# A streaming-encoder block on one core: one more of eight weight pieces per FFN group by seven products, and some down weights' low parts made by accumulating transfers

## The chip, the core and the metric

The kernel runs on one core of a Trainium2 chip. The metric is device time in microseconds, the median of several executions. One further execution is recorded by the hardware profiler; it gives the trace from which all rows here are copied. Engines: PE is TensorE (matrix products; PEld its weight loads), DVE is VectorE, ACT is ScalarE, POOL is GpSimd, SP is SyncE, which here issues the loads. An engine's name with a q is its queue of DMA issues.

## The reference

One layer over 256 tokens with 2048 features, all in float32:

```python
for l in range(DEPTH):
    x = x + 0.5 * swiglu(rms_norm(x, ffn1_norm[l]), ffn1_w_up[l], ffn1_w_down[l])
    h = rms_norm(x, mix_norm[l])
    proj = h @ w_in[l]
    ...
    x = x + merged @ w_out[l]
    x = x + cross_attention(rms_norm(x, xattn_norm[l]), rms_norm(mem, mem_norm[l]),
                            xattn_wq[l], xattn_wkv[l], xattn_wo[l])
    x = x + 0.5 * swiglu(rms_norm(x, ffn2_norm[l]), ffn2_w_up[l], ffn2_w_down[l])
return rms_norm(x, final_norm)

def swiglu(h, w_up, w_down):
    gate, up = jnp.split(h @ w_up, 2, axis=-1)
    return (jax.nn.silu(gate) * up) @ w_down
```

The change concerns the two FFNs (`swiglu`): 2048 features to 2 x 5632 columns, and 5632 back to 2048.

## The kernel before

**Split operands.** A float32 matrix operand is used as two float32r parts: the high part is a rounded copy (`split`, line 120, on ScalarE) and the low part the difference from the original (line 121, on VectorE). A product of two such operands is made of three TensorE products, high by high, low by high and high by low (`three`, lines 449, 450 and 452).

**Groups and pieces.** The 5632 hidden columns are 11 groups of 512. The up weights of a group come in eight pieces of 1 MB (128 x 2048), one for each pair of feature tiles; a piece holds four blocks of 512 columns: two feature tiles, each with its up and its gate columns. A piece is used in one of these ways (`PRODUCTS`):
- plain (group 0): eight block products by three, 24 TensorE products;
- mixed: also eight block products, added into the same sums as the fast pieces;
- fast: seven block products (21 TensorE products) in the manner of Winograd's form of Strassen's scheme. VectorE first makes differences of the blocks into a tile `td` (lines 213 to 215), ScalarE copies three blocks of the piece and four of `td` to float32r, and VectorE makes the low parts (`l`, and `tl` in two halves).

The activations have matching sums and differences (`operand_pairs` and `sums`): "less" for a mixed pair, "sums" for a fast one, and both for the pairs in `BOTH`.

The down weights of a group are four pieces of 24 products. After each group's up pieces stand down pieces of earlier groups: two after groups 1 and 2, four after groups 3 to 10 (two blocks of two output columns: c0 b0, c0 b1, c1 b0, c1 b1, and likewise c2, c3 after the next group), and eight at the end (`ffn_order`). Groups 3 to 10 have the same pattern of 12 pieces and are called steady groups here.

**How a piece gets ready** (`weights`, `begin_added`, `prepare`). The list `plan` holds every piece in order of use. Each call of `weights` prepares the piece after the one that TensorE is about to use. `prepare` loads the piece into `raw` and splits it. A mixed piece with the kind "added" takes another way: its load is issued one piece earlier, ScalarE writes the negated rounded copy into `l` (line 191), and GpSimd issues a transfer that adds `raw` to `l` (line 192). So VectorE has nothing to do for it, ScalarE two passes, and the raw buffer stays taken until that transfer has landed. Before the change the kind "added" goes to the mixed pieces from group 3's second on, 15 in each FFN.

**Buffers.** `raw`, `h` and `l` are rings of three buffers; a fast piece takes two of `h` (the copies of the piece and of `td`). `td`, `tl` and the group's sums `ev` share a ring of three ("wide"). A buffer is written again when all uses of its last content are done. TensorE's sums are in eight banks.

**End of a group** (in `ffn`). Seven sums are put together from the banks: a copy on ScalarE (line 533), then seven additions on VectorE (lines 534 to 545), two SiLUs on ScalarE (line 481) and two products with the up part on VectorE (line 482). Four pieces later the result is transposed on TensorE (`turn`, line 489), copied and split. A pair of down pieces ends with two residual sums (line 561).

**Order.** Every engine has one instruction stream, in which a scheduler puts the instructions when the kernel is built; within an engine that order is fixed, and each instruction waits for its operands and buffers. In the first eight pieces the order is that of the code (`manual_schedule`); there `head` and `rest` hang other work behind certain pieces: loading x, the sums of squares for the first normalisation (`head_residual`, `sq1`, line 352), its square root (`head_rstd`), and the sums for the activations.

Of the kernel before, what the change touches and what calls it, by code (L numbers as in the profile page):

```python
# [13 lines left out]
P = 128  # L14
# [5 lines left out]
NG = DFF // 512  # L20
# [21 lines left out]
def ffn_order():  # L42

    out, down = [("plain", 0, p) for p in range(8)], [("down", 0, 1, c, 0) for c in range(4)]
    for g in range(1, NG):
        if g < 3:  # L50
            out += [(("mixed", "fast")[p % 2], g, p) for p in (0, 1, 2, 3, 5, 4, 7, 6)]
        else:
            out += [("mixed" if p in (0, 6) else "fast", g, p) for p in (1, 3, 0, 4, 2, 6, 5, 7)]
        if g > 2 and g % 2:
            down = [("down", g - 2, 2, c, b) for c in range(4) for b in (g - 2, g - 1)]
        n = 2 if g < 3 else 4
        out, down = out + down[:n], down[n:]
    return out + [("down", NG - 2, 2, c, b) for c in range(4) for b in (NG - 2, NG - 1)]
# [3 lines left out]
def block_kernel(ctx: ExitStack, tc: tile.TileContext, xT, xin, memT, vec, gfin, bgate, lruw, wu1, wd1, win, wv,  # L62
                 wg, wab, wout, wq, wk, wvm, wo, wu2, wd2, out_):
    nc = tc.nc
    pe, dve, act, sp = nc.tensor, nc.vector, nc.scalar, nc.sync
# [21 lines left out]
    def slot(dt=F32, name="slot"):  # L87
        return slots.tile([P, 1024], dt, name=name, tag="slot")
# [12 lines left out]
    def col(name, i=0, n=1):  # L101
        a = VEC[name][0] + i
        return vt[:, a:a + n]
# [8 lines left out]
    xt = [const.tile([P, 4 * T], F32, name=f"x{q}") for q in range(4)]  # L112
# [6 lines left out]
    def split(h, l, raw):  # L119
        done["high"] = act.activation(h, raw, ACT.Copy).ins  # L120
        dve.tensor_tensor(out=l, in0=raw, in1=h.bitcast(F32), op=ALU.subtract)  # L121
# [4 lines left out]

    plan, ahead = [], []
    orders = dict.fromkeys(("ffn1", "ffn2"), ffn_order())

    def plan_ffn(name, wu, wd):  # L130
        for e in orders[name]:
            src = wd[e[4], e[3]] if e[0] == "down" else wu[e[1], e[2]]
            kind = "fast" if e[0] == "fast" else "added" if e[0] == "mixed" and e[1:] > (3, 0) else "plain"
            plan.append(((name,) + e, src, kind))

    def plan_columns(name, w, which):
# [2 lines left out]
    def plan_rows(name, w, g):  # L139
        plan.extend(((name, g, kq), w[g, kq], "plain") for kq in range(w.shape[1]))  # L140

    plan_ffn("ffn1", wu1, wd1)
    for hf in range(2):
        for base in (8, 0):
# [11 lines left out]
    for name, w in (("mv", wvm), ("o", wo)):  # L156
        for g in range(4):
            plan_rows(name, w, g)
    plan_ffn("ffn2", wu2, wd2)

    head, rest = [], {}
# [238 lines left out]

    BOTH = [2, 4]
    xd = []

    def operand_pairs(src, gain, q, xg, out):

        for a in src:
            i = len(out)
            g = xg[:, i * 512:(i + 1) * 512]  # L410
            for z in range(2):
                act.activation(g[:, z * T:][:, :T], a[:, z * T:(z + 1) * T], ACT.Copy,
                               scale=col(gain, 4 * q + 2 * i + z))
            h, l = slot(F32R, "xh"), slot(F32R, "xl")
            split(h[:, :512], l[:, :512], g)
            less = None if i else (h[:, 512:768], l[:, 512:768])
            if 2 * q + i in BOTH:
                if 2 * q + i == BOTH[0]:
                    xd.append(slot(F32R, "xd"))
                n = 512 * BOTH.index(2 * q + i)  # L420
                less = [xd[-1][:, a:a + 256] for a in (n, n + 256)]
            out.append(((h, l), less))

        def sums(which=((0, "less"), (0, "sums"), (1, "less"), (1, "sums"))):
            s = slot(name="xs")
            for i, ((h, l), less) in enumerate(out):
                a = [xg[:, i * 512 + j * P:][:, :P] for j in range(4)]

                def made(h, l, n, at, terms):
                    o = [s[:, at + j * P:][:, :P] for j in range(n)]  # L430
                    for j, (x, y, op) in enumerate(terms(o)):
                        dve.tensor_tensor(out=o[j], in0=x, in1=y, op=op)
                    split(h, l, s[:, at:at + n * P])

                if less and (i, "less") in which:
                    made(*less, 2, 0, lambda o: ((a[0], a[1], ALU.subtract), (a[2], a[3], ALU.subtract)))
                if (i or 2 * q in BOTH) and (i, "sums") in which:
                    if not i and len(which) > 1:
                        s = slot(name="xs")
                    made(h[:, 512:], l[:, 512:], 4, 512 * i,  # L440
                         lambda o: ((a[1], a[3], ALU.add), (o[0], a[0], ALU.subtract),
                                    (a[1], a[0], ALU.subtract), (a[2], o[1], ALU.subtract)))

        return sums
# [126 lines left out]
    pairs1, sq1 = [], TokenSquares()  # L571

    xq, sums1 = {}, []

    def head_x(p):

        q = p // 2
        if p % 2 == 0:
            xq[q] = slot(name="xf"), slot(name="xg"), []
        src, xg, out = xq[q]  # L580
        a = p % 2 * 512
        sp.dma_start(src[:, a:a + 512], xT[:, p * 512:(p + 1) * 512])
        sums = operand_pairs([src[:, a:a + 512]], "ffn1_norm", q, xg, out)
        if p % 2:
            sums1.append(sums)
        pairs1.append(out[-1])

    def head_residual(i):
        for c in (2 * i, 2 * i + 1):
            for t in range(2):  # L590
                sp.dma_start(xt[c][:, t * 512:(t + 1) * 512], xin[t * P:(t + 1) * P, c * 512:(c + 1) * 512])
            sq1.add(c)
        if i:
            sp.dma_start(vt[:, small_n:NVEC], vec[:, small_n:])

    head += [lambda p=p: head_x(p) for p in range(8)]
    for i in range(2):
        rest[4 + i] = lambda i=i: head_residual(i)
    rstd1 = []

    def head_rstd():
        rstd1.append(sq1.rstd_tokens())
        act.activation(rstd1[0][:, 2:], rstd1[0][:, :1], ACT.Silu)

    for q, i in enumerate((3, 6, 7, 9)):
        rest[i] = lambda q=q: sums1[q](((0, "less"), (1, "sums")))
    rest[8] = head_rstd
    for q, i in ((1, 17), (2, 18)):
        rest[i] = lambda q=q: sums1[q](((0, "sums"),))


# [415 lines left out]
    for g in range(4):  # L1027
# [4 lines left out]
        for t in range(2):  # L1032
            s = slot(F32R, "vs")
            f = scoped["tmp2"].tile([P, 512], F32, name="vf", tag="part")
# [18 lines left out]
    def to_ffn(c):  # L1053
        out = []
        sums2.append(operand_pairs(turned(xt[c]), "ffn2_norm", c, slot(name="xg"), out))
        pairs2.extend(out)
        if c < 2:
            sums2.pop(0)()
# [130 lines left out]
```

## Time and profile before

| | |
|---|---|
| median of 3 runs | 2455.01 us (2454.0 to 2455.87) |
| profiled execution | 2456.57 us, its span in the trace 2454.8 us |
| TensorE, VectorE, ScalarE busy | 99%, 77%, 57% of the span |
| granted TensorE clock, mean | 0.997 |
| HBM read | 472.07 MB |
| adding transfers (line 192) | 30, median 7.3 us from issue to landing |

In a row of the timeline the columns are start, duration, engine, line, operation, output and inputs, and in brackets the engine's idle time before it with what ended it. A group's row gives busy time, the mean of one in ns, and the idle time in front. x with a number counts instructions. Records of products overlap: the spacing of their starts tells their cost. Windows give busy time of each engine in a stretch.

### The profile page before, as it was taken

The numbers are of one execution on the slowest core, as the hardware profiler recorded it, in microseconds if no ns is written. First come the engines' busy times: TensorE is split into PE (matmuls) and PEld (weight loads), VectorE is DVE, ScalarE is ACT, GpSimd is POOL, SyncE is SP. The second block draws the span as 40 slices with busy tenths as digits, with TensorE's granted clock in tenths as the row PEclk, the third lists the DMA queues.
The fourth block names the chain that finished last, engine by engine and source line by source line (L and its number), as shares of the span: only waits on it lengthen the run. The fifth ranks groups of instructions, "written<-read, shape, count | busy, mean of one in ns | idle before, by whom it ended". The sixth has DMA issues, their size and how long they took to land.

```text
span 2454.8 us, 30191 instructions
## 1 busy us (share of the span) xinstructions
PE 2434.6 (99%) x12250; PEld 2036.9 (83%) x12250; DVE 1894.1 (77%) x2016; ACT 1391.2 (57%) x1398; POOL 28.3 (1%) x36
## 2 busy tenths in 40 slices
PE   9999999999999999999999999999999999999998
PEld 7887888888888888888888888888888788888887
DVE  6998999999865757567665676556689999999995
ACT  7555666666564454477434554555555566666664
POOL 0000000000000000000000000000000000000000
PEclk9999999999999999999999999999999999999999
DMA  7557777777655445546555555444555677777774
GB/s 278 190 203 234 248 235 235 234 239 239 223 183 194 173 172 180 174 166 228 194 188 177 210 198 189 172 172 155 189 189 189 209 238 239 240 240 235 235 235 152
DMA packets 75020, 507.59 MB, mean 207 GB/s; under 512 B 8320, under 2 KB 8576, under 8 KB 15232
## 3 DMA queue, kind: packets, MB, share of 16 engines
q1 hardware_dynamic: 69840, 473.06, 53.4%
q0 software_dynamic: 4320, 31.46, 6.4%
q8 instruction: 96, 1.57, 0.2%
q10 hardware_dynamic: 720, 1.13, 0.1%
q14 instruction: 44, 0.36, 0.0%
HBM read 472.07 MB, written 2.10 MB: 193 GB/s over the span
## 4 chain that ended last, share of the span: by engine, by line
PE 95%; DVE 2%; ACT 1%; DMA 1%; issue 0%; SPq 0%; ACTq 0%; DVEq 0%
PE acc L449 17%; PE acc L450 17%; PE acc L452 17%; PE acc L231 11%; PE acc L252 8%; PE acc L253 8%; PE acc L255 8%; PE acc L235 5%; DMA raw<-wu 1%; PE acc L489 1%; ACT h L120 1%; DVE l L121 1%; PE acc L389 1%; PE acc L765 0%; PE acc L1048 0%; PE acc L1003 0%
## 5 line engine op out<-in xcount | busy, mean ns | idle before, releaser
L121 DVE TENSOR_TENSOR l<-raw,h 128x2048 fp32r<-128x2048 f32 (+2 forms) x422 | 878.0, 2087 | 364.5 <-ACT h L120 353.0
L120 ACT ACTIVATE h<-raw 128x2048 fp32r<-128x2048 f32 (+2 forms) x422 | 736.7, 1753 | 637.5 <-PE acc L253 204.8
L449 PE MATMUL acc<-h,xh 128*128 128x512 f32 x1280 | 501.2, 392 | 7.1 <-ACT h L120 7.0
L450 PE MATMUL acc<-h,xl 128*128 128x512 f32 x1280 | 499.7, 391 | 0.0
L120 ACT ACTIVATE h<-td 128x1024 fp32r<-128x1024 f32 x224 | 229.6, 1055 | 178.4 <-PE acc L450 131.0
L252 PE MATMUL acc<-h,ops 128*128 128x512 f32 x832 | 326.9, 393 | 0.0
L253 PE MATMUL acc<-h,ops 128*128 128x512 f32 x832 | 324.3, 390 | 0.0
L121 DVE TENSOR_TENSOR tl<-td,h 128x1024 fp32r<-128x1024 f32 x224 | 267.4, 1221 | 33.6 <-ACT h L120 31.0
L449 PEld LDWEIGHTS acc<-h,xh 128*128 128x128 f32 x1280 | 241.7, 189 | 60.0 <-ACT h L120 9.7
L450 PEld LDWEIGHTS acc<-h,xl 128*128 128x128 f32 x1280 | 241.9, 189 | 50.1
L231 PE MATMUL acc<-ops,h 128*128 128x512 f32 x1152 | 278.0, 393 | 0.3
L449 PE MATMUL acc<-h,hidop 128*128 128x512 f32 x704 | 275.7, 392 | 0.0
L450 PE MATMUL acc<-h,hidop 128*128 128x512 f32 x704 | 274.3, 390 | 0.0
L231 PEld LDWEIGHTS acc<-ops,h 128*128 128x128 f32 x1152 | 211.9, 188 | 42.9 <-DVE ops L292 0.9
L452 PE MATMUL acc<-l,xh 128*128 128x512 f32 x832 | 218.9, 390 | 0.0
L255 PE MATMUL acc<-l,ops 128*128 128x512 f32 x832 | 206.1, 390 | 0.0
L452 PE MATMUL acc<-l,hidop 128*128 128x512 f32 x704 | 188.3, 389 | 0.0
L452 PEld LDWEIGHTS acc<-l,xh 128*128 128x128 f32 x832 | 156.5, 188 | 32.6
L255 PEld LDWEIGHTS acc<-l,ops 128*128 128x128 f32 x832 | 156.2, 188 | 32.4
L252 PEld LDWEIGHTS acc<-h,ops 128*128 128x128 f32 x832 | 156.2, 188 | 32.3
L253 PEld LDWEIGHTS acc<-h,ops 128*128 128x128 f32 x832 | 156.3, 188 | 31.6
L452 PEld LDWEIGHTS acc<-l,hidop 128*128 128x128 f32 x704 | 132.2, 188 | 27.5
(220 smaller groups left out, 2347.6 us busy)
## 6 DMA issues: line engine op xcount, KB each, us to landing
raw<-wu SPq DMA_DIRECT2D x172, 1024.0 KB, 4.8
raw<-wd SPq DMA_DIRECT2D x88, 1024.0 KB, 4.8
raw<-win SPq DMA_DIRECT2D x40, 1024.0 KB, 4.8
raw<-wg SPq DMA_DIRECT2D x32, 1024.0 KB, 4.8
l<-raw POOLq DMA_DIRECT2D x30, 1024.0 KB, 7.3
raw<-wab SPq DMA_DIRECT2D x16, 1024.0 KB, 4.8
raw<-wout SPq DMA_DIRECT2D x16, 1024.0 KB, 4.8
raw<-wq SPq DMA_DIRECT2D x16, 1024.0 KB, 4.8
```

Source lines behind the costliest of these rows:

```text
L120: done["high"] = act.activation(h, raw, ACT.Copy).ins
L121: dve.tensor_tensor(out=l, in0=raw, in1=h.bitcast(F32), op=ALU.subtract)
L231: pe.matmul(acc, h[:, k * P:(k + 1) * P], xs[k], start=k == 0, stop=False)
L235: done["product"] = pe.matmul(acc[:, :T], l[:, k * P:(k + 1) * P], xs[k][:, :T], start=False, stop=k == KT - 1).ins
L252: pe.matmul(accs[t], x[:, t * P:][:, :P], h[j], start=first and j == 0, stop=False)
L253: pe.matmul(accs[t], x[:, T + t * P:][:, :P], h[j], start=False, stop=False)
L255: done["product"] = pe.matmul(accs[t], x[:, t * P:][:, :P], l[j], start=False, stop=last and j == 3).ins
L389: pe.transpose(accs[m // 2][:, m % 2 * T + t * P:][:, :P], tile[:, t * 512 + m * P:][:, :P], ident)
L449: pe.matmul(acc, ah, bh, start=start, stop=False)
L450: pe.matmul(acc, al, bh, start=False, stop=False)
L452: pe.matmul(acc, ah, bl, start=False, stop=stop)
L489: pe.transpose(acc[:, z * T + t * P:][:, :P], hid[t][:, (2 * y + z) * P:][:, :P], ident)
```

## The change

In groups 1 and 2 of each FFN pair 4 turns from mixed to fast (mixed are then 0, 2 and 6), in groups 3 to 10 pair 0 (mixed is then only 6, and it stands fourth). The kind "added" goes to every mixed piece but pair 0 and to two down pieces in each four behind groups 3 to 10: the first and the last of the four. `BOTH` names pairs 0 and 2, and pair 4, now only fast, has its sums where its "less" was. The order of loads into the ring of three follows `begin_added` as before. In the first pieces the residual's four chunks are loaded and squared one behind each of pieces 4 to 7 instead of two behind each of pieces 4 and 5, and the sums for the activations move.

```diff
-            out += [(("mixed", "fast")[p % 2], g, p) for p in (0, 1, 2, 3, 5, 4, 7, 6)]
+            out += [("mixed" if p in (0, 2, 6) else "fast", g, p) for p in (0, 1, 2, 3, 5, 4, 7, 6)]
         else:
-            out += [("mixed" if p in (0, 6) else "fast", g, p) for p in (1, 3, 0, 4, 2, 6, 5, 7)]
+            out += [("mixed" if p == 6 else "fast", g, p) for p in (1, 3, 0, 6, 4, 2, 5, 7)]
...
-            kind = "fast" if e[0] == "fast" else "added" if e[0] == "mixed" and e[1:] > (3, 0) else "plain"
+            kind = "fast" if e[0] == "fast" else "plain"
+            if e[0] == "mixed" and e[2]:
+                kind = "added"
+            if e[0] == "down" and 0 < e[1] < NG - 2 and (e[3] + e[4] - e[1]) % 2 == 0:
+                kind = "added"
...
-    BOTH = [2, 4]
+    BOTH = [0, 2]
+    FAST = [4]
...
-            less = None if i else (h[:, 512:768], l[:, 512:768])
+            less = None if i or 2 * q in FAST else (h[:, 512:768], l[:, 512:768])
...
-                if (i or 2 * q in BOTH) and (i, "sums") in which:
-                    if not i and len(which) > 1:
+                if (i or 2 * q in BOTH + FAST) and (i, "sums") in which:
+                    if not i and less and len(which) > 1:
...
-    def head_residual(i):
-        for c in (2 * i, 2 * i + 1):
-            for t in range(2):
-                sp.dma_start(xt[c][:, t * 512:(t + 1) * 512], xin[t * P:(t + 1) * P, c * 512:(c + 1) * 512])
-            sq1.add(c)
-        if i:
+    def head_residual(c):
+        for t in range(2):
+            sp.dma_start(xt[c][:, t * 512:(t + 1) * 512], xin[t * P:(t + 1) * P, c * 512:(c + 1) * 512])
+        sq1.add(c)
+        if c == 3:
...
-    for i in range(2):
-        rest[4 + i] = lambda i=i: head_residual(i)
...
-    for q, i in enumerate((3, 6, 7, 9)):
-        rest[i] = lambda q=q: sums1[q](((0, "less"), (1, "sums")))
-    rest[8] = head_rstd
-    for q, i in ((1, 17), (2, 18)):
+    for i in range(3):
+        rest[4 + i] = lambda i=i: head_residual(i)
+    for q, i in enumerate((3, 7, 8, 9)):
+        rest[i] = lambda q=q: sums1[q](((0, "sums" if 2 * q in FAST else "less"), (1, "sums")))
+    made = rest[7], rest[8]
+    rest[7] = lambda: [f() for f in (lambda: head_residual(3), made[0])]
+    rest[8] = lambda: [f() for f in (head_rstd, made[1])]
+    for q, i in ((0, 22), (1, 24)):
         rest[i] = lambda q=q: sums1[q](((0, "sums"),))
```

## The prediction

> **What bounds the kernel now.** I read the page first (busy times, then the chain of work that ended last), then the waits of TensorE, then stretches of one group of the FFN.
>
> ```profile
> span 2454.8 us, 30191 instructions
> PE 2434.6 (99%) x12250; PEld 2036.9 (83%) x12250; DVE 1894.1 (77%) x2016; ACT 1391.2 (57%) x1398; POOL 28.3 (1%) x36
> ...
> PE 95%; DVE 2%; ACT 1%; DMA 1%; issue 0%; SPq 0%; ACTq 0%; DVEq 0%
> ...
> PE acc L449 <- ACT h L120: 7.0, 4, 3.0
> PE acc L452 <- DVE tl L121: 3.0, 1, 3.0
> ```
>
> TensorE is busy 2434.6 of 2454.8 us and waits only 10 us for anybody: products set the end, so taking products away pays unless another engine takes over. VectorE's 77% hides two kinds of stage. The stretches below (columns: time, PE, weight loads, VectorE, ScalarE, GpSimd, then granted clock, DMA share, GB/s) show FFN groups 1, 2 and a steady group, each cut at its transposes:
>
> ```profile
> 61.62:114.45 52.83, 52.83 (x237) 43.54 (x236) 52.43 (x64) 29.93 (x28) 0.00 (x0) 1.00 0.56 199
> 114.45:166.35 51.90, 51.90 (x235) 43.06 (x233) 50.71 (x50) 27.64 (x24) 0.00 (x0) 1.00 0.55 203
> ...
> 286.57:348.67 62.10, 62.10 (x280) 51.50 (x278) 57.35 (x56) 38.38 (x32) 1.76 (x2) 1.00 0.73 237
> ...
> 286.57 1.03 PE L489 MATMUL acc<-vt,ev 128*128 128x128 f32 x8
> ...
> 348.67 1.03 PE L489 MATMUL acc<-vt,ev 128*128 128x128 f32 x8
> ```
>
> In the FFN VectorE works 92 to 99% of the time, so it is a near second bound there. The added FFN work lands on it; that decides this case.
>
> **The change part by part.** *Products.* Each group from 1 to 10 of both FFNs has one mixed piece (24 products) fewer and one fast piece (21) more. A steady group is 6x21 + 2x24 + 4x24 = 270 products and eight transposes. Taking about 0.8 us for the transposes (1.03 less the overlap of the last with what follows), (62.10 - 0.8)/270 = 0.227 us a product (the 0.39 us of one record is latency; they overlap). Three fewer are 0.68 us a group: a floor of 61.42 us, and 20 x 0.68 = 13.6 us in all if nothing else happens.
>
> *VectorE in a steady group (3 to 10).* The groups of its instructions in one period (393.19 to 455.28, columns busy, mean ns, idle before):
>
> ```profile
> L121 DVE TENSOR_TENSOR tl<-td,h 128x1024 fp32r<-128x1024 f32 x12 | 14.2, 1221 | 2.2 <-ACT h L120 2.0
> L121 DVE TENSOR_TENSOR l<-raw,h 128x1536 fp32r<-128x1536 f32 x6 | 10.5, 1756 | 1.3 <-PE acc L452 0.7 <-ACT h L120 0.6
> L121 DVE TENSOR_TENSOR l<-raw,h 128x2048 fp32r<-128x2048 f32 x4 | 9.1, 2288 | 0.9 <-ACT h L120 0.9
> L213 DVE TENSOR_TENSOR td<-raw 128x1024 f32<-128x1024 f32 x6 | 7.3, 1218 | 0.0
> L215 DVE TENSOR_TENSOR td<-raw,td 128x512 f32<-128x512 f32 x6 | 4.1, 691 | 0.2
> L214 DVE TENSOR_TENSOR td<-raw,td 128x512 f32<-128x512 f32 x6 | 4.1, 690 | 0.1
> ...
> ACT h L120 <- PE acc L450: 19.8, 12, 3.9
> ```
>
> A fast piece costs 1.22 + 0.69 + 0.69 + 1.76 + 2x1.22 = 6.8 us; the mixed piece it replaces was an adding transfer and cost VectorE nothing. Two of four down pieces become adding transfers: minus 2 x 2.29 = 4.6. So 57.4 + 6.8 - 4.6 = 59.6 us busy against a floor of 61.42: 1.8 us is left, where the group before had 2.2 + 1.3 + 0.9 + 0.3 = 4.7 us of idle.
>
> *A new wait at the group's end.* The weights' copies come from rings of three buffers. With the added down pieces the order is down A, P, P, A. The negated copy of the second A reuses the low buffer of the first A, so it waits until TensorE has ended the first A. In the changed kernel's instruction order on ScalarE this copy stands behind the group's first eviction and ahead of the high copy for the second P and of both SiLUs, and on VectorE the two gate products that need the SiLUs stand ahead of the second P's low part. The durations from the group's end before:
>
> ```profile
> 397.16 0.39 PE L449 MATMUL acc<-h,hidop 128*128 128x512 f32 x1
> ...
> 399.88 0.39 PE L449 MATMUL acc<-h,hidop 128*128 128x512 f32 x1
> ...
> 397.60 0.68 DVE L534 TENSOR_TENSOR ev<-acc,ev 128x512 f32<-128x512 f32 x1
> ...
> 401.92 1.41 DVE L482 SCALAR_TENSOR_TENSOR ev<-ev,rtok 128x512 f32<-128x512 f32 x2
> ...
> 399.17 1.92 ACT L120 ACTIVATE h<-raw 128x2048 fp32r<-128x2048 f32 x1 [3.72 <-PE acc L450]
> ...
> 400.99 1.32 ACT L481 ACTIVATE ev<-ev,rtok 128x512 f32<-128x512 f32 x2
> ...
> 411.06 1.90 ACT L191 ACTIVATE l<-raw 128x2048 fp32r<-128x2048 f32 x1
> ```
>
> Half a down piece is 2.72 us (397.16 to 399.88). Let E be the end of the group's last up product; TensorE's order puts the first half of the first A ahead of it, so that piece ends at E+2.7. Allowing 0.2 us for a wait to pass on: negated copy to E+4.8, high copy to E+6.7, first SiLU to E+7.4. VectorE starts its seven eviction sums at E+0.2, needs 4.3 us (397.60 to 401.92) and is done at E+4.5: it stands still for 2.9 us. Gates to E+8.8, low part of the second P (2.2) to E+11.0. TensorE needs it after the first P and eight products: E + 2.7 + 5.45 + 1.8 = E+9.95. It stalls 1.1 us. Behind the waiting copy on ScalarE also queue the high copies of the next group, behind the gates on VectorE its residual sums and differences.
>
> Two ways of counting meet: TensorE 61.42 + 1.1 = 62.5, VectorE 59.6 + 2.9 = 62.5. That is the lower end. The upper end keeps all 4.7 us of the old idle as well: 67.2. I take 0.9 of the 4.7: 3.5 was ended by ScalarE's copies, and ScalarE itself had waited 19.8 us for TensorE to release buffers; when VectorE is the late one these releases come early, and only the passing to and fro stays. So 63.4 us a group, 1.3 over before, in 16 groups: +20.8 us (ends: +0.4 and +5.1 a group).
>
> *Groups 1 and 2.* Of four mixed pieces three leave VectorE (two by adding transfers, one as fast): +6.8 - 3x2.29 = -0.1 us, and VectorE was at 50.7 to 52.4 of 52 us. No gain: 0 (ends: -2.7, all four savings, and +4).
>
> *Transfers.* One more adding transfer a steady group, with two more ScalarE passes: 38.4 + 3.6 (copies of a fast piece) - 3.8 + 3.8 = 42 of 61 us, covered.
>
> ```profile
> l<-raw POOLq DMA_DIRECT2D x30, 1024.0 KB, 7.3
> raw<-wu SPq DMA_DIRECT2D x172, 1024.0 KB, 4.8
> ...
> 178.49 10.33 DMA raw<-wu
> ```
>
> The DMA share of group 2, without adding transfers, is 0.55 of 51.9 us; of a steady group with two 0.73 of 62.1. With ten loads at 2.85 us there and twelve here, one adding transfer is some (45.3 - 34.2)/2 = 5.5 us: the third takes the share to about 0.83. Its cost is 0 in my sum; the second A lands at E+4.8+7.3 = E+12.1, 3 us ahead of TensorE's use of it (E + 2.7 + 10.9 + 1.8 = E+15.4). SP's next load into the first A's raw buffer waits for that piece's accumulation, and the loads behind it queue; the third row, a load that took 10.3 us beside the first adding transfer, is the price if this cover goes (a rival below).
>
> *Head.* Squares come in twos behind each of four x chunks instead of four and four:
>
> ```profile
> 42.09 0.66 PE L449 MATMUL acc<-h,xh 128*128 128x512 f32 x1 [2.50 <-ACT h L120]
> 42.55 0.63 PE L450 MATMUL acc<-h,xl 128*128 128x512 f32 x1
> 42.98 0.63 PE L449 MATMUL acc<-h,xh 128*128 128x512 f32 x1
> ...
> 50.59 0.50 PE L449 MATMUL acc<-h,xh 128*128 128x512 f32 x1 [1.17 <-ACT h L120]
> 50.93 0.39 PE L450 MATMUL acc<-h,xl 128*128 128x512 f32 x1
> ...
> 1928.36 0.73 PE L452 MATMUL acc<-tl,xh 128*128 128x512 f32 x2 [3.03 <-DVE tl L121]
> ...
> 1930.28 0.63 PE L450 MATMUL acc<-h,xl 128*128 128x512 f32 x1
> 1930.70 0.63 PE L449 MATMUL acc<-h,xh 128*128 128x512 f32 x1
> ```
>
> Two stalls (2.50 + 1.17) are at stake, and eight products at 0.43 us instead of 0.23 after the longer one (42.55 to 42.98), 1.6 us. The square root and its table load still stand there, and the sums of three chunks now come together: I take -3 (ends -5.3 and +2). The 3 us stalls at the first adding transfers of each FFN I leave as they are: 0 (ends -9 and +5).
>
> *The clock.* A gap of 1.17 us left the next products at 0.23 us, gaps of 2.50 and 3.03 us were followed by products 0.43 us apart. The Trainium skill (TensorE: Matmul & The Clock Gate, section "Part 1: The HAM clock gate (the "warmup" mystery)") puts the drop to half rate behind an idle window of about 3.4 us; by it none of my stalls would cost clock. The 2.50 us gap here disagrees, but a 1.1 us stall is below all of them, so the sum is the same by both unless stalls double.
>
> *Sum.* 20.8 + 0 + 0 - 3 = +18 us. The profiled execution took 2456.57 us (span 2454.8 and 1.8 around it), 1.6 over the median of 2455.01; 2456.57 + 18 is 2474.4, and against the median 2473.
>
> **The rivals.**
> A, the savings arrive: VectorE's 59.6 us fit into 61.42 if ScalarE's blocked copy is passed early, because VectorE enters the group's end ahead. For it: TensorE never waited on a steady group before. Against it: VectorE can't run ahead past a gate product. Deciding point: VectorE's stand at the gates under 1 us. Price: -13.6 - 3, 2438 us. This is the one on the other side. Chance 0.10.
> B, only the forced stall remains and all old idle goes: 62.5 a group, 16 x 0.4 - 3, 2458 us. For it: nearly all of the old idle ended with copies that waited for TensorE. Against: differences and copies still go to and fro. Chance 0.14.
> C, loads come late: the accumulations hold raw buffers, a load of the next group's second piece arrives as late as the 10.3 us one, and each steady group has a 3.0 us stall with eight products at half speed: 61.42 + 3.0 + 1.6 = 66.0, 16 x 3.9 - 3 = +60, 2515 us. For it: three loads queue behind one accumulation. Against: 7.3 us is the usual landing, and E+12.1 is in time. Chance 0.08.
> That the order of pieces doesn't bring the fewer products is excluded by the diff's lists.
>
> **How the numbers follow.** The forecast (a steady group of 63 to 65 us) has the other 0.68: 2473 us, own range 2464 to 2496. To hold 8 in 10 with half of A left out and most of C, the range is 2450 to 2498. A measurement tells about 0.2% (5 us) from no change. Faster: A and a little of B with a good head, 0.13; the same: half of B, 0.07; slower 0.80.
>
> **What would show it.** Each step: a steady group from transpose to transpose of 63.4 us (62.1 before), 59.6 us of VectorE in it; on VectorE an idle of 2 to 3 us ahead of the gate products, ended by the SiLU on ScalarE; on ScalarE the negated copy of a down piece ended by TensorE; on TensorE a stall of about 1 us at a down piece's low products. Wrong if groups fall to 61.4 (A), if stalls name loads (C), or if group 1 or 2 moves by more than 2 us.

## The result, and the profile after

The changed kernel takes 2516.65 us (median of 4 runs, 2513.18 to 2518.43) beside 2454.93 for the kernel before (2454.0 to 2455.87): a ratio of 1.0247, interval 1.0234 to 1.026. It is slower, as forecast, but by three times as much, and outside the range. The page of the changed kernel, with its waits of TensorE (us in total, times, longest):

```profile
span 2515.0 us, 30284 instructions
PE 2449.9 (97%) x12190; PEld 2027.6 (81%) x12190; DVE 1911.8 (76%) x2094; ACT 1473.8 (59%) x1464; POOL 50.8 (2%) x62
...
PE 64%; DMA 16%; DVE 11%; issue 5%; ACT 4%; SPq 0%; DVEq 0%; ACTq 0%; POOLq 0%
...
PE acc L454 <- ACT h L120: 42.6, 36, 3.2
...
PE acc L457 <- DMA l<-raw: 2.8, 2, 2.1
```

VectorE's share fell by a point, ScalarE's rose by two, to 59%. In the chain that ended last, DMA went from 1% to 16% and VectorE from 2% to 11%: TensorE now waits 42.6 us for ScalarE's copies, and the chain leads from these to loads and adding transfers. TensorE itself hardly waits for a transfer (2.8 us). The queue of loads does, because a load needs a raw buffer that a transfer still reads (waits in us in total, times, longest; first the changed kernel, then the kernel before):

```profile
SPq L214 <- DMA l<-raw: 326.3, 34, 12.0
```

```profile
SPq L207 <- DMA l<-raw: 38.0, 14, 4.7
SPq L210 <- DMA l<-raw: 23.6, 8, 9.1
```

The transposes that open a period show where. First the changed kernel, then the kernel before (its first is at 61.62, in the prediction):

```profile
55.97 1.03 PE L494 MATMUL acc<-vt,ev 128*128 128x128 f32 x8
234.06 1.03 PE L494 MATMUL acc<-vt,ev 128*128 128x128 f32 x8
693.11 1.03 PE L494 MATMUL acc<-vt,ev 128*128 128x128 f32 x8
1833.35 0.82 PE L494 MATMUL acc<-vt,ev 128*128 128x128 f32 x6
1995.71 1.03 PE L494 MATMUL acc<-vt,ev 128*128 128x128 f32 x8
2456.25 1.03 PE L494 MATMUL acc<-vt,ev 128*128 128x128 f32 x8
```

```profile
224.45 1.04 PE L489 MATMUL acc<-vt,ev 128*128 128x128 f32 x8
659.13 1.03 PE L489 MATMUL acc<-vt,ev 128*128 128x128 f32 x8
1799.49 1.04 PE L489 MATMUL acc<-vt,ev 128*128 128x128 f32 x8
1961.39 1.03 PE L489 MATMUL acc<-vt,ev 128*128 128x128 f32 x8
2396.05 1.03 PE L489 MATMUL acc<-vt,ev 128*128 128x128 f32 x8
```

| stretch | before | after | difference |
|---|---|---|---|
| start to the first transposes | 61.62 | 55.97 | -5.7 |
| first FFN, first to fourth transposes | 162.8 | 178.1 | +15.3 |
| second FFN, the same | 161.9 | 162.4 | +0.5 |
| both FFNs, fourth to eleventh: 14 steady groups | 14 x 62.10 | 14 x 65.69 | +50.2 |
| sum, beside the difference of the spans | | | +60.3 (60.2) |

A steady group took 65.7 us (64.3 to 68.3), not 63.4. The next rows show two stretches (time, PE, weight loads, VectorE, ScalarE, GpSimd, clock, DMA share, GB/s): group 2 of the first FFN, then one steady group. Below them stand the DMA issues of the steady group (count, KB, median us to landing):

```profile
110.31:171.79 61.48, 54.93 (x231) 44.31 (x230) 52.76 (x62) 34.31 (x30) 1.25 (x2) 0.94 0.58 200
...
496.33:560.89 64.56, 62.48 (x276) 50.55 (x275) 58.64 (x59) 41.99 (x35) 2.59 (x3) 1.00 0.77 236
```

```profile
raw<-wu SPq DMA_DIRECT2D x9, 1024.0 KB, 6.4
raw<-wd SPq DMA_DIRECT2D x4, 1024.0 KB, 7.2
l<-raw POOLq DMA_DIRECT2D x3, 1024.0 KB, 11.1
```

Group 2 took 61.5 us where it was 51.9, at a clock of 0.94. In the steady group VectorE has 58.6 us of work, 1 less than I counted, and 5.9 us of idle. The median of its three adding transfers is 11.1 us, where the sum had 7.3 for the second down piece: piece 6's took 11.4 us, the down pieces' 7.9 and 11.1. This group is at the upper end. Over the 14 steady groups piece 6's transfer took 11.4 to 12.3 us in twelve, the first down piece's 7.9 to 9.5 and the second's 7.9 to 11.1. The chain through this group says how late landings become idle time:

```profile
505.70 11.41 DMA l<-raw
517.10 0.02 SPq L214
517.16 4.75 DMA raw<-wu
...
522.00 1.23 DVE td L217
...
541.27 1.92 ACT h L120
...
546.82 11.05 DMA l<-raw
```

Piece 6's transfer lands at 517.10 and frees its raw buffer; that very moment SP sends the load of piece 2, the third to take a buffer after it. It lands at 521.9. VectorE has idled (1.38 us by its own timeline) and then works back to back from 522 to 541. Being late, it frees its own buffers late: the load of the first plain down piece leaves at 533.83, behind a fast piece's last difference, and takes 7.3 us, so ScalarE's copy of it comes only at 541.27. The second adding transfer of a down piece starts at 546.82 and holds the buffer that piece 3 of the next group waits for.

### The profile page after: what moved, and what is told of

It reads as the page before. It is cut to its first block, busy times and chain, and to the rows that moved or that the text cites. A ratio compares the mean times of both kernels' runs of the same rounds, so it can differ in the third digit from the quotient of the medians.

```text
span 2515.0 us, 30284 instructions
## 1 busy us (share of the span) xinstructions
PE 2449.9 (97%) x12190; PEld 2027.6 (81%) x12190; DVE 1911.8 (76%) x2094; ACT 1473.8 (59%) x1464; POOL 50.8 (2%) x62
## 4 chain that ended last, share of the span: by engine, by line
PE 64%; DMA 16%; DVE 11%; issue 5%; ACT 4%; SPq 0%; DVEq 0%; ACTq 0%; POOLq 0%
PE acc L235 11%; PE acc L454 8%; PE acc L256 8%; PE acc L257 8%; PE acc L259 8%; PE acc L455 7%; PE acc L457 7%; DMA raw<-wu 6%; DMA l<-raw 6%; PE acc L239 5%; DMA raw<-wd 4%; ACT h L120 3%; DVE tl L121 3%; DVE l L121 3%; DVE td L217 2%
## 5 line engine op out<-in xcount | busy, mean ns | idle before, releaser
L121 DVE TENSOR_TENSOR l<-raw,h 128x2048 fp32r<-128x2048 f32 (+2 forms) x396 | 809.2, 2046 | 386.3 <-ACT h L120 380.5
L120 ACT ACTIVATE h<-raw 128x2048 fp32r<-128x2048 f32 (+2 forms) x396 | 679.7, 1719 | 579.6 <-PE acc L257 205.9
L454 PE MATMUL acc<-h,xh 128*128 128x512 f32 x1260 | 499.2, 398 | 46.7 <-ACT h L120 42.6
L455 PE MATMUL acc<-h,xl 128*128 128x512 f32 x1260 | 490.9, 393 | 0.0
L120 ACT ACTIVATE h<-td 128x1024 fp32r<-128x1024 f32 x264 | 275.1, 1054 | 197.2 <-PE acc L455 75.8
L121 DVE TENSOR_TENSOR tl<-td,h 128x1024 fp32r<-128x1024 f32 x264 | 319.3, 1220 | 20.3 <-ACT h L120 20.0
L454 PE MATMUL acc<-h,hidop 128*128 128x512 f32 x704 | 279.1, 396 | 0.0
L455 PE MATMUL acc<-h,hidop 128*128 128x512 f32 x704 | 277.7, 394 | 0.0
L457 PE MATMUL acc<-l,xh 128*128 128x512 f32 x732 | 198.0, 390 | 1.8 <-DVE l L121 1.8
L217 DVE TENSOR_TENSOR td<-raw 128x1024 f32<-128x1024 f32 x132 | 160.9, 1219 | 25.4 <-DMA raw<-wu 24.6
```

Source lines behind the costliest of these rows:

```text
L217: dve.tensor_tensor(out=two[0], in0=raw[:, None, :512].broadcast_to([P, 2, 512]), in1=two[1], op=ALU.subtract)
L454: pe.matmul(acc, ah, bh, start=start, stop=False)
L455: pe.matmul(acc, al, bh, start=False, stop=False)
L457: pe.matmul(acc, ah, bl, start=False, stop=stop)
```

## The experiments

Theory 1: three raw buffers are too few for three adding transfers a group. Theory 2, the rival nearest to my forecast: the sum of VectorE's work and the order of instructions at the group's end set the time, and the transfers are harmless. A third question is what the head does by itself. Two runs take one thing out of the changed kernel each, and one puts the head alone into the kernel before. The most direct test of theory 1, a fourth raw buffer with nothing else changed (x1_raw4), has no time: the wide ring needs 24 KB a partition and would have 22.8 left. It comes below as x6_raw4s, which gives up two slots for the buffer.

**x2_nodown: all down pieces plain.**

```diff
-            if e[0] == "down" and 0 < e[1] < NG - 2 and (e[3] + e[4] - e[1]) % 2 == 0:
-                kind = "added"
```

> The changed kernel with all four down pieces of a group as plain ones, their low parts on VectorE as before the change; the one more fast piece and the head stay. Theory 1 (held raw buffers): the second and third accumulation of a group are gone, and with them the late loads; VectorE then has 57.4 + 6.8 = 64.2 us of work in a group and bounds it at 64.2 to 66 us; the time is 2450 + 16 x 2.1 to 16 x 3.9 us, 2483 to 2512 us, plus what groups 1 and 2 cost. Theory 2 (VectorE's work plus 6 us of idle that belongs to the order of instructions, transfers harmless): 64.2 + 6.1 = 70 us a group, about 2585 us, much slower than the changed kernel.

2502.8 us, ratio 1.0194 (1.0179 to 1.021). Steady groups 65.1 us:

```profile
358.00:422.70 64.70, 62.95 (x277) 50.58 (x276) 62.43 (x62) 38.95 (x32) 0.88 (x1) 1.00 0.63 211
```

VectorE works 62.4 of 64.7 us and bounds the group; with the load on it up by 3.8 us the idle went down by 3.6. So the 5.9 us of idle in the changed kernel do not belong to the order of instructions: theory 2 wanted 70 us here. This run also takes passes from ScalarE, so by itself it can't clear the order; the next one keeps every pass. The extra fast piece needs relief for VectorE, and the adding transfers do give that; they cost about as much elsewhere.

**x3_noadd: the down pieces' transfers left out, their copies kept.**

```diff
-        nc.gpsimd.dma_start(l, raw, accum_op=ALU.add)
+        if add:
+            nc.gpsimd.dma_start(l, raw, accum_op=ALU.add)
```

(`add` is true for mixed up pieces alone. The kernel leaves out the addition, so the low parts of the added down pieces keep only the negated copy.)

> The changed kernel without the accumulating transfers of the down pieces: ScalarE's high and negated copies stay, but nothing is added, so the low parts of those pieces are wrong values and this part of the computation is left out. The work of every engine and its order stay the same. Theory 1 (held raw buffers and the transfers' 11 us): the raw buffers of down pieces are free when ScalarE is done; a steady group falls to 61.5 to 63.5 us and the time to 2450 to 2480 us. Theory 2 (order and VectorE's sum): a steady group stays near 65.7 us, the time above 2505 us.

2468.12 us, ratio 1.0047 (1.0033 to 1.0061); steady groups 63.0 us:

```profile
353.30:416.30 63.00, 62.23 (x276) 50.60 (x275) 58.64 (x59) 42.09 (x35) 0.88 (x1) 1.00 0.65 217
```

The same 58.64 us of VectorE, and 2.7 us less a group. The two transfers of down pieces cost this; the sum had missed 2.3 us. That is theory 1's side. Group 2 of the first FFN, behind which no down piece is added, stayed at 61.9 us. What is left of the loss starts, in the chain of this group, at piece 6's transfer, which lands as late as in the changed kernel:

```profile
362.71 11.51 DMA l<-raw
```

So its length isn't due to the down pieces' transfers. In x2 it took 7.9 us; what makes it long here was not separated.

**x4_head: the kernel before with the new head alone.**

```diff
-    def head_residual(i):
-        for c in (2 * i, 2 * i + 1):
+    def head_residual(c):
...
+    for i in range(3):
+        rest[4 + i] = lambda i=i: head_residual(i)
+    for q, i in enumerate((3, 7, 8, 9)):
```

> The kernel before with only the head of the changed one: squares in twos behind each x chunk, the sums of pairs in their new places. From the two traces the first transposes come 5.65 us earlier in the changed kernel (55.97 against 61.62). If the head does this by itself: 2449.3 us, 0.9977 of before. If the FFN's first loads or the squares only move the wait (the head's gain is given back at the first group): within 1 us of 2455.

2451.01 us, ratio 0.998 (0.9971 to 0.9989), first transposes at 56.19. Both head stalls are gone, and most of the gain is kept. This part of the change is worth 4.6 us alone (2.7 to 7.1 by the interval).

Is it the transfer that holds the raw buffer, or its share of the DMA engines, or the number of buffers? Two runs:

**x5_dram: the transfers read device memory.**

```diff
-        nc.gpsimd.dma_start(l, raw, accum_op=ALU.add)
+        nc.gpsimd.dma_start(l, src, accum_op=ALU.add)
```

> The changed kernel with one word different: the accumulating transfers read the weight piece a second time from device memory instead of from the raw buffer, so a raw buffer is free when ScalarE has made its two copies. Number, size and time of the transfers stay. Run x3_noadd (no transfers for down pieces, 63.0 us a steady group) still had the chain transfer of piece 6, then the load that waited for its raw buffer, in every group, and lost 10 us in group 2 of the first FFN. Theory 1 (it is the holding of the raw buffer): those waits go too; a steady group is 61.4 to 62.8 us, group 2 of the first FFN is back near 52 to 54, the time is 2436 to 2462 us. Theory 1b (it is the transfers' share of the DMA engines that makes loads late, wherever they read from): 65 to 67 us a group and 2505 to 2525 us. The forecast's forced wait at the group's end, if it appears once loads are early: 62.5 to 63.4 us a group, 2455 to 2475 us, with VectorE idle ahead of the gate products.

2509.92 us, ratio 1.0221 (1.0206 to 1.0236); steady groups 65.6 us, no better than the change itself. (The 64.8 us for this kernel in two later expectations is a mean that took in an earlier, shorter interval.) So theory 1 in its first form, the transfer as the only holder, fell, and both numbers are those of theory 1b. What happens instead, in the waits of the queue of loads, in the chain and in the timeline of TensorE:

```profile
SPq L214 <- ACT h L204: 236.0, 33, 13.7
```

```profile
465.05 0.70 DVE td L219
465.80 8.02 DMA raw<-wd
```

```profile
476.83 0.79 PE L454 MATMUL acc<-h,xh 128*128 128x512 f32 x1 [2.09 <-ACT h L120]
477.42 0.63 PE L455 MATMUL acc<-h,xl 128*128 128x512 f32 x1
477.85 0.63 PE L454 MATMUL acc<-h,xh 128*128 128x512 f32 x1
```

The added piece's buffer has another holder: loads that waited for the transfer now wait for the piece's late high copy on ScalarE (line 204), about as often. The load of the first plain down piece again leaves when a fast piece's last difference has freed a buffer, takes 8.0 us beside the transfers, and TensorE stands for 2.1 us.

**x6_raw4s: four raw buffers.**

```diff
-    rawp = pool("raw", 3)
+    rawp = pool("raw", 4)
-    slots = pool("slots", 24)
+    slots = pool("slots", 22)
```

> The changed kernel with four raw buffers for loads, paid for by 22 instead of 24 of the 4 KB slots (the part between the FFNs may run differently by that; the steady groups are read by themselves). Theory 1 (held raw buffers): as with the transfers from device memory, a steady group falls from 65.7 to 61.4 to 63 us, and the time by 16 x 2.7 to 16 x 4.2 = 43 to 68 us to 2449 to 2474, give or take the middle. Theory 1b (share of the DMA engines): 65 to 66 us a group, as the transfers still take the same 11 us each. Theory 2 (order at the group's end): 65 to 66 us.

2454.53 us, ratio 0.9999 (0.9989 to 1.0008); steady groups 62.06 us. A group, and its issues:

```profile
410.30:472.40 62.10, 62.02 (x277) 50.70 (x276) 58.72 (x59) 41.94 (x35) 2.60 (x3) 1.00 0.81 259
```

```profile
raw<-wu SPq DMA_DIRECT2D x9, 1024.0 KB, 6.8
raw<-wd SPq DMA_DIRECT2D x4, 1024.0 KB, 6.6
l<-raw POOLq DMA_DIRECT2D x3, 1024.0 KB, 10.2
```

Loads and transfers land about as late as in the changed kernel and the DMA engines are busier (0.81), but TensorE is busy for 62.02 of the 62.10 us. In the steady groups late landings cost nothing once a load can leave earlier. All 3.6 us a group, and 10.7 of the 15.3 us at the start of the first FFN, are gone with a fourth raw buffer. Theory 1b falls with that: it wanted 65 to 66 us.

**x7_before_raw4: the control, four raw buffers (and 22 slots) in the kernel before.**

> Control: the kernel before with four raw buffers and 22 slots, nothing of the change. Theory 1 says that the buffers matter only for the changed kernel, since here TensorE sets the end of a steady group (62.1 us, 273 products at 0.223 us and eight transposes): steady groups stay at 62.1 us, the time at 2453 to 2458 us. Rival: the fourth buffer is worth time in any kernel (the changed one got faster by it for a reason that has nothing to do with the change): steady groups under 61.8, the time under 2450 us.

2447.4 us, ratio 0.9965 (0.9951 to 0.9979). The steady groups are unchanged at 62.1, as theory 1 says (they hold 270 products, not the 273 of the expectation). The time isn't: it is below theory 1's range, because the interval with the first adding transfers is some 52 us in both FFNs, where it was 58.1 and 57.0. In the first FFN:

```profile
168.20:220.10 51.90, 51.90 (x234) 42.98 (x233) 50.95 (x49) 32.36 (x27) 1.00 (x1) 1.00 0.70 243
```

The 3 us stalls there, which I left as they were, had the same cause already before the change.

**x8_order4: x6_raw4s with the up pieces in the old order.**

```diff
-            out += [("mixed" if p == 6 else "fast", g, p) for p in (1, 3, 0, 6, 4, 2, 5, 7)]
+            out += [("mixed" if p == 6 else "fast", g, p) for p in (1, 3, 0, 4, 2, 6, 5, 7)]
```

> The changed kernel with four raw buffers (as x6_raw4s) and the up pieces of groups 3 and later in the order they had before the change (1, 3, 0, 4, 2, 6, 5, 7), the one adding piece later. x6_raw4s ran 62.0 us a steady group with no stall of TensorE over 0.2 us, 0.6 above the floor of 61.4, in two or three hesitations around pieces 2, 5 and 7, three fast pieces in a row with two high copies each. If these come from three in a row: 61.4 to 61.8 us a group and 2444 to 2451 us. If they come from VectorE's and ScalarE's passing to and fro as such: 62 us and 2454. If the adding piece now lands too late beside the first down piece's: 62.5 to 64 us.

2459.09 us, ratio 1.0014 (1.0005 to 1.0023), above both times expected. Steady groups 62.0 us: twelve of 14 take 61.9, the first of each FFN 62.9. The old order brings at most 0.2 us a group, so three fast pieces in a row are not the main source of the hesitations. 62.0 us is what passing to and fro as such would give, but that isn't shown by it.

**x9_dram_early_high and x12_early_high: the high copy of an added piece directly behind its negated copy**, with the transfer from device memory and from the raw buffer.

```diff
         nc.gpsimd.dma_start(l, src, accum_op=ALU.add)
-        return raw, l
+        h = hp.tile([P, 2048], F32R, name="h", tag="h")
+        done["high"] = act.activation(h, raw, ACT.Copy).ins
+        return h, l
...
-            raw, l = begun.pop(0)
-            h = hp.tile([P, 2048], F32R, name="h", tag="h")
-            done["high"] = act.activation(h, raw, ACT.Copy).ins
-            return h, l
+            return begun.pop(0)
```

> x5_dram (the accumulating transfers read device memory) with the high copy of an added piece made directly behind its negated copy, so its raw buffer is free some 7 us earlier; transfers and loads are the same. If the time that a raw buffer is occupied is the cause, whoever occupies it: a steady group falls from 64.8 to 62 to 63.5 us, the time to 2455 to 2480 us. If it is the loads' own slowness beside the transfers (8 us instead of 5): no change, 64 to 66 us, 2500 to 2515 us. If the high buffer, taken earlier, becomes the next shortage (three of them, a fast piece uses two): slower than x5_dram, over 66 us a group.

> The changed kernel with the high copy of an added piece directly behind its negated copy, the transfers reading the raw buffer as in the change. With the changed kernel (65.7 us a steady group), x5_dram (64.8) and x9_dram_early_high (61.8 undisturbed) this fills the fourth corner: two things hold a raw buffer, the transfer until it lands and the late high copy. If both must go (the transfer alone holds it long enough): 64 to 66 us a group and 2500 to 2520 us, like the changed kernel. If the late high copy is the one that matters, whatever the transfer reads: 61.8 to 63 us a group and 2455 to 2480 us.

2471.97 us (ratio 1.0065, 1.0051 to 1.0079) and 2478.22 us (1.0087, 1.007 to 1.0104). Steady groups, means of 14:

| | high copy late | high copy early |
|---|---|---|
| transfer reads the raw buffer | 65.7 (the change) | 63.1 (x12) |
| transfer reads device memory | 65.6 (x5) | 62.4 (x9) |

An undisturbed group of x9:

```profile
421.70:483.50 61.80, 61.75 (x277) 50.82 (x276) 58.55 (x60) 41.98 (x35) 2.62 (x3) 1.00 0.80 253
```

Both times are in the ranges expected for the late high copy as what matters (x12's 63.1 us is just above the 63 named for a group). Its place is worth 2.6 to 3.2 us, what the transfer reads 0.1 to 0.7. In x12 the early copy doesn't free the raw buffer, since the transfer still holds it; loads wait for the transfers as much as in the changed kernel:

```profile
SPq L213 <- DMA l<-raw: 332.5, 34, 13.3
```

So most of x12's gain has another source. The nearest is ScalarE's order, where a 1.9 us copy no longer stands between the copies that VectorE and TensorE wait for; no run shows which of these hand-overs it is. Most of the 3.6 us thus needs both, three raw buffers and the late copy: a fourth buffer takes all of it away, an earlier copy 2.6.

**x11_dram_early_high_raw4: x9 with four raw buffers and 22 slots.**

> x9_dram_early_high (61.8 us in its undisturbed steady groups, with 1 to 6 us stalls in single intervals of the first FFN) with four raw buffers and 22 slots. If occupied raw buffers still cause those single stalls: all steady groups 61.8, no interval over 62.6, 2441 to 2452 us. If the stalls come from an accumulating transfer that lands late (up to 6.2 us of waiting for one): they stay, 2458 to 2475 us.

2471.9 us, ratio 1.0064 (1.0051 to 1.0076). The first theory missed, the second held: steady groups stay at 62.4, and the stalls left over are mostly waits of TensorE for transfers that land late (15.6 us in three waits, the longest 6.8). A fourth buffer is no help against those.

**x10_head_raw4: the kernel before with the new head and four raw buffers.**

> The kernel before with the head of the changed one (as x4_head) and four raw buffers with 22 slots (as x7_before_raw4), no change in the FFNs. x4_head was 4.6 us faster than before (first transposes at 56.2 instead of 61.6), x7_before_raw4 8.3 us (the intervals with the first adding transfers 51.9 and 52.1 instead of 58.1 and 57.0, 1 us given back in the middle, 1.7 at the start). If the two gains are separate: 2455.7 - 4.6 - 8.3 = 2443 us, first transposes at 56 to 58. If the head's gain depends on the three buffers: 2447 us.

2441.61 us, ratio 0.9942 (0.9929 to 0.9956). The two gains add up, and this beats both kernels. TensorE's waits, over the whole span:

```profile
PE warm L109 <- DVE ones L106: 1.1, 1, 1.1
PE acc L870 <- ACT i L871: 0.4, 1, 0.4
PE acc L1017 <- DVE st L1011: 0.2, 1, 0.2
```

Nothing in the FFNs makes TensorE wait any more.

Beside x6_raw4s (same head, same buffers) it also prices the FFN part of the change with enough raw buffers: 12.9 us slower, as the steady groups gain nothing (62.06 to 62.1) and the first three intervals of the FFNs lose 10.2 and 4.5 us (167.4 and 161.3 us beside 157.2 and 156.8). No run takes these early intervals apart. In x6 TensorE waits there 5.4 us for VectorE's low parts and 2.8 for adding transfers in the first FFN, 0.7 and 2.6 in the second; the changed kernel has such transfers from group 1 on, the kernel before from group 3.

## Why the prediction was right in its direction and wrong in its size

- **The direction** was right, but with luck: the wait at the group's end that carried it isn't there (below). The floor came out nearly: x9's undisturbed groups took 61.8 us against 61.42. That VectorE has little room was right too: 58.6 us were measured against 59.6.
- **The step that failed** is the one on the transfers: "Its cost is 0 in my sum". The prediction saw that loads queue behind an accumulation and called that covered. It tested the cover only for TensorE's use of the second down piece, and that held (2.8 us of such waits in the whole run). What wasn't covered is the loads: their queue waited 326.3 us for transfers at the line of the fast pieces alone, where it had waited some 62 us in all before. The term is worth 2.7 us a group by x3, and with three raw buffers the change lost 3.6 (x6). The landing times were too short as well. The 7.3 us are the page's median over all 30 transfers; the medians in the steady groups of before are 7.1 to 8.5 us (10.8 in the first, where it cost nothing), in this one 8.0:

```profile
raw<-wu SPq DMA_DIRECT2D x8, 1024.0 KB, 5.4
raw<-wd SPq DMA_DIRECT2D x4, 1024.0 KB, 5.9
l<-raw POOLq DMA_DIRECT2D x2, 1024.0 KB, 8.0
```

 In the group shown for the changed kernel they are 11.1 us, and the loads take 6.4 and 7.2. The DMA share that I worked out (0.83) was near what x6 shows (0.81), but a share below 1 was no cover: with three raw buffers loads left too late for their longer landing.
- **The forced wait** at the group's end, which carried most of my +1.3 us, isn't there. "The negated copy of the second A reuses the low buffer of the first A, so it waits until TensorE has ended the first A" is wrong. ScalarE, VectorE and TensorE at the end of the group shown above:

```profile
544.51 1.91 ACT L195 ACTIVATE l<-raw 128x2048 fp32r<-128x2048 f32 x1
```

```profile
551.03 0.68 DVE L550 TENSOR_TENSOR ev<-acc,ev 128x512 f32<-128x512 f32 x1
551.63 1.41 DVE L487 SCALAR_TENSOR_TENSOR ev<-ev,rtok 128x512 f32<-128x512 f32 x2
```

```profile
545.89 1.07 PE L457 MATMUL acc<-l,hidop 128*128 128x512 f32 x4
...
549.10 1.07 PE L457 MATMUL acc<-l,hidop 128*128 128x512 f32 x4
```

 The negated copy runs at 544.51, before TensorE reads the first A's low part (545.89 and 549.10), so it writes another buffer; nothing waits at the gates (551.63 follows 551.03 at once). That 63.0 us without the transfers (x3) is close to my 63.4 is no proof of that step: the loss that remained there began at piece 6's transfer.
- **Rival C** had the kind of the cause (loads late behind accumulations) and, by its 66.0 us, the size; I gave it 0.08. Its price was right partly by chance: instead of one 3.0 us stall in each group, TensorE waits for ScalarE's copies 36 times, 1.2 us on average, and only 4 of the 14 groups lie above 67 us. My argument against it was the 7.3 us landing.
- **Groups 1 and 2**: 0 was right in the second FFN (+0.5 with the interval behind them) and wrong in the first (+15.3, of which group 2 has 9.6), against an upper end of +4 a group. With four buffers 10.7 of it are gone: there too loads came late (a load of 10.4 us stood in the chain).
- **Head**: -3 was the safe middle; both stalls went, -5.7, a little beyond my end of -5.3.
- **Three products fewer**: 0.68 us a group was the floor's gain, and x6, x8 and x9 realised 0.04 to 0.3 of it. Where the rest went is open; that seven fast pieces leave no slack where TensorE, VectorE and ScalarE hand over is my reading and wasn't shown.

## What to carry to other kernels

A buffer ring has to cover the landing time under the new load, not under the old one. When a change adds transfers, take the landing times from one stage of the trace, not from the page's median, and ask for each load which buffer it waits for and since when; the waits of the queue of loads say it. A share of busy DMA engines of about 0.8 was no cover here. Look also at the order on the engine that makes the copies: with three buffers, one copy put earlier gave back 2.6 of the 3.6 us. Before adding work to relieve an engine, give the ring one more buffer in the unchanged kernel: here that (with two slots fewer) brought 8.3 us.

## What was not expected of the hardware

TensorE dropped to half rate after shorter gaps than the prediction knew: in x5 a gap of 2.09 us was followed by products 0.43 us apart (477.42 to 477.85 above). But the length of a gap doesn't decide it alone: in x2 one of 3.21 us was followed by products 0.23 us apart:

```profile
577.34 0.51 PE L452 MATMUL acc<-h,xh 128*128 128x512 f32 x1 [3.21 <-ACT h L120]
577.68 0.40 PE L453 MATMUL acc<-h,xl 128*128 128x512 f32 x1
577.91 0.40 PE L452 MATMUL acc<-h,xh 128*128 128x512 f32 x1
```

The Trainium skill (TensorE: Matmul & The Clock Gate, section "Part 1: The HAM clock gate (the "warmup" mystery)") names an idle window of about 3.4 us as the condition; here 2.09 us sufficed, so the measurement speaks against taking that figure as a safe limit.
